# The last join of a triangular inverse: four quadrant products per head rewritten as products over all 128 rows and columns, with one kept tile

## The chip, the core and the metric

The kernel runs on one core of one Trainium2 chip, in one launch. The metric is the time of that launch in device microseconds, the lower the better. Before the change three runs gave 2576.31, 2579.31 and 2580.29 us; the median is 2579.31 us.

Five engines take part, each with its own instruction queue worked off in order: TensorE (PE in the profile; its weight loads are listed apart as PEld), VectorE (DVE), ScalarE (ACT), GpSimd (POOL), and SyncE (SP), which issues the DMA transfers. They meet through semaphores: an instruction that needs another engine's result waits in its queue until the semaphore has the value.

## What is computed

One layer of a hybrid network over 128 context tokens and 2048 latent tokens (17 tiles of 128), width 1024: a normalised and modulated input goes through one projection into a gated DeltaNet in two directions (4 heads of 128) and a gated MLP over groups, then through an output projection, and after that through a squared-ReLU MLP of width 4096. The change touches the DeltaNet alone. The reference solves a unit lower triangular system for each chunk and head:

```python
k_beta = k * beta
a_mat = jnp.where(strict, jnp.einsum('bnhcd,bnhsd->bnhcs', k_beta, k) * decay, 0.0)
rhs = jnp.concatenate([v * beta, k_beta * jnp.exp(g)[..., None]], axis=-1)
sol = lax.linalg.triangular_solve(a_mat + jnp.eye(DN_CHUNK, dtype=f32), rhs,
                                  left_side=True, lower=True, unit_diagonal=True)
```

The kernel works on chunks of 128 tokens and forms the inverse of this matrix itself, with matrix products.

## The kernel before

The work falls into three stretches. Up to about 430 us the kernel projects the tokens, convolves and normalises queries and keys, and writes them and their products to DRAM. From there to about 1230 us it runs the DeltaNet scan with the remaining projections between its steps. The rest is the MLP, almost all of it 128x512 products on PE (helper `mm3`, L220 to L222: each product of two float32 matrices is done as three products of high and low parts).

**The scan.** There are 34 units (one tile of 128 tokens in one direction: context forward and backward, 16 latent tiles forward, 16 backward), each with four heads. `unit` has the steps that follow the state from unit to unit ("chain"). Two successive units form a `pair`, and `pair` holds the steps that need no state ("prep"): the inverse for the eight heads of the pair at once. So there are 17 pairs; only the first mixes directions, and in the other 16 all eight heads have the same one.

**The inverse.** `AH` is minus the system matrix in half precision, and `AL` what half precision left out. `X` and `Y` are the approximate inverse and its transpose, built up from diagonal blocks: `firsts` starts with blocks of 2, and `level(w)` for w = 2, 4, 8, 16, 32 joins neighbouring blocks of w to blocks of 2w. A level is two steps. The first multiplies `AH` with half of the columns of `Y` (L1173: eight products, each with a 128x128 stationary operand and 64 moving columns) and DVE puts the result under a mask into the tile `P` of that level (L1176). The second multiplies `X` with `P` (L1187) and `P` with `X` (L1193), eight products each, again 128x128 with 64 moving columns, and ACT copies both results back into `Y` and `X` (L1196).

The last join, from blocks of 64 to the whole 128, is written apart, and on quadrants. `rows[d]` names for direction d the half `ra` and the half `rb` of the rows. Step one (L1212) multiplies the 64x64 quadrant `AH[rb, ra]` with the 64x64 quadrant `Y[rb, rb]`, and ACT copies the result into the first 64 columns of a fresh tile `Pm` (L1215). Step two multiplies the quadrant `X[ra, ra]` with `Pm` (L1224) and `Pm` with `X[ra, ra]` (L1228); ACT copies the first into `Y` (L1231) and DVE the second into `X` (L1232). Two more steps follow: the residual `R` of the inverse in full precision (L1240 to L1242), and one correction with it into `T` (L1249 to L1251), which the chain uses. `Pm` and `R` are two tiles in turn in the same buffer, which has one slot (tag "R").

**The order.** Every step has a due time in units; `emit` writes them down sorted by it, and projection work ("fill") is placed between chain and prep steps. PE executes that list in order: in most places six 128x512 products stand between one step of the chain or the inverse and the next, long enough for the copy that the next step needs.

Of the kernel before, what the change touches and what calls it, by code (L numbers as in the profile page):

```python
# [62 lines left out]
def hybrid_step(  # L63
# [7 lines left out]
    V, A, G, T = nc.vector, nc.scalar, nc.gpsimd, nc.tensor  # L71
# [73 lines left out]
    def bc4(ap):  # L145
        return ap.unsqueeze(1).to_broadcast([P, 4, P])
# [780 lines left out]
    with ExitStack() as ph:  # L927
# [8 lines left out]
        def pd():  # L936
            return psd.tile([P, 4, P], F32, tag="d", name="pd", bufs=4)
# [7 lines left out]
        def pd8():  # L945
            return psd.tile([P, 8, 64], F32, tag="d", name="pd", bufs=4)

        def f16(tag):
            return pp.tile([P, 8, P], F16, tag=tag, name=tag, bufs=1)
# [12 lines left out]
        def clear(lo, hi):  # L962
            for pm in pms.values():
                V.tensor_copy(pm[:, lo:hi], ident16.unsqueeze(1).to_broadcast([P, hi - lo, P]))

        clear(0, 8)

        def behind(fn, name):

            start = len(tc.nc.cur_bb.bb.instructions)  # L970
            fn()
            for x in tc.nc.cur_bb.bb.instructions[start:]:
                tc.add_manual_dep(x, name, mybir.DependencyInfo(
                    mybir.DependencyClass.NoSync, mybir.DependencyReason.DATA), reason="order")
# [144 lines left out]
        def pair(us):  # L1119

            g = {}
            ds = [u["d"] for u in us]
            spans = [(0, 8, ds[0])] if ds[0] == ds[1] else [(0, 4, ds[0]), (4, 8, ds[1])]
# [4 lines left out]
            def mine(name, c):  # L1128
                return g[name][:, 4 * c : 4 * c + 4, :]
# [73 lines left out]
            rows = {d: (slice(64 * d, 64 * d + 64), slice(64 - 64 * d, P - 64 * d)) for d in (0, 1)}  # L1203

            @steps.append
            def _():
                p = pd8()
                g["Pm"] = f16("R")
                for lo, hi, d in spans:
                    ra, rb = rows[d]  # L1210
                    for h in range(lo, hi):
                        T.matmul(p[ra, h, :], g["AH"][rb, h, ra], g["Y"][rb, h, rb], start=True, stop=True)  # L1212
                for lo, hi, d in spans:
                    ra, rb = rows[d]
                    A.copy(g["Pm"][ra, lo:hi, 0:64], p[ra, lo:hi, :])  # L1215

            @steps.append
            def _():
                py, px = pd8(), pd8()
                pm = g["Pm"]  # L1220
                for lo, hi, d in spans:
                    ra, rb = rows[d]
                    for h in range(lo, hi):
                        T.matmul(py[ra, h, :], g["X"][ra, h, ra], pm[ra, h, 0:64], start=True, stop=True)  # L1224
                for lo, hi, d in spans:
                    ra, rb = rows[d]
                    for h in range(lo, hi):
                        T.matmul(px[rb, h, :], pm[ra, h, 0:64], g["X"][ra, h, ra], start=True, stop=True)  # L1228
                for lo, hi, d in spans:
                    ra, rb = rows[d]  # L1230
                    A.copy(g["Y"][ra, lo:hi, rb], py[ra, lo:hi, :])  # L1231
                    V.tensor_copy(g["X"][rb, lo:hi, ra], px[rb, lo:hi, :])  # L1232

            @steps.append
            def _():
                g["R"] = f16("R")
                for c in range(2):
                    p = pd()
                    for h in range(H):
                        T.matmul(p[:, h, :], mine("AH", c)[:, h, :], mine("Y", c)[:, h, :], start=True, stop=False)  # L1240
                        T.matmul(p[:, h, :], mine("AL", c)[:, h, :], mine("Y", c)[:, h, :], start=False, stop=True)
                    V.tensor_tensor(out=mine("R", c), in0=p, in1=bc4(ident16), op=ALU.add)  # L1242
# [619 lines left out]
    rows = {}  # L1862
# [7 lines left out]
    def final(t, y):  # L1870

        ga = gate_rows(0) if t == 0 else rows["ga"]
        x = [fetch(x2_d[t * P : (t + 1) * P, n * 512 : n * 512 + 512], "x") for n in range(2)]
        ss = smp.tile([P, 2], F32, tag="ss2", name="ss2")
        half_out(y, 1, x, ga, ss)

        def rest():
            half_out(y, 0, x, ga, ss)
            r = smp.tile([P, 1], F32, tag="r", name="r")
            add(ss[:, 0:1], ss[:, 0:1], ss[:, 1:2])  # L1880
            rsqrt_cols(r, ss[:, 0:1], 1, 1.0 / D, EPS)
            for n in range(2):
                V.scalar_tensor_tensor(out=y[n], in0=y[n], scalar=r, in1=rows["nf"][n], op0=ALU.mult, op1=ALU.mult)
                store(out=yrow(t)[:, n * 512 : n * 512 + 512], in_=y[n])

        return rest
# [88 lines left out]
    for j, t in enumerate(range(8, -1, -1)):  # L1975
        st = h2_steps(t, bank, lambda: junk16, w512, own=own_tile if t == 0 else None)
        p = 16 + 19 * j // 2
# [43 lines left out]
    for m, (n, i, u, q) in enumerate(todo):  # L2021
# [6 lines left out]
        if q == 0:  # L2028
            ps = bank()
            if i == 4:  # L2030
                rest = final(pairs[u][1], [acc["v", u], acc["q", u]])
            elif i == 2:
                rest = final(0, [y0[0], y0[1]]) if u == 8 else final(pairs[u][0], [acc["x", u], acc["u", u]])
        h, lo = sops.pop(m)
# [75 lines left out]
```

## Time and profile before

| what | value |
|---|---|
| three runs | 2576.31, 2579.31, 2580.29 us |
| span of the profiled execution, first to last instruction | 2574.7 us |
| PE busy in the span | 2542.1 us, 99%, 15296 products |
| DVE, ACT, POOL busy | 1781.9, 1192.5, 313.9 us |
| mean granted TensorE clock | 0.999 |
| first and last start of L1212, L1224, L1228 | 494.7 and 1182.0 us |

The page lists no time of the profiled execution beside its span. The span is 4.6 us below the median of the runs (0.18%) and 1.6 us below the fastest of them, so it belongs to a run like these, and what an execution holds ahead of its first and behind its last instruction is small. In the timeline each row has the start and the length in us, the engine, the source line, the result and the operands, the rows and columns of the array that the stationary operand takes (64\*64, 128\*128), the shape of the moving operand and its type, and the number of instructions merged into the row; a bracket has the idle time before it and what ended it. A product is pipelined, so its length overlaps the next one: what PE spends on it is the distance from its start to the next start.

### The profile page before, as it was taken

To read this page: it belongs to the slowest core of one execution; us is meant where nothing else is said; L and a number is where in the kernel's file an instruction comes from. 1 tells how busy PE (TensorE), PEld (TensorE's weight loads), DVE (VectorE), ACT (ScalarE), POOL (GpSimd) and SP (SyncE) were. 2 spreads that over 40 slices of the span, in tenths; PEclk is the share of its full clock that TensorE was granted. 3 is DMA by queue.
4 is the path that set the end of the run, shared out by engine and by line. 5 is a ranking of instruction groups with operands and counts; after the bars stand their busy time and mean duration, and the time that the engine had idled before them with its cause. 6 is when DMAs were issued, how large, how long until landed. Compare 5 with 4: busy or idle time off the path is not lost.

```text
span 2574.7 us, 43713 instructions
## 1 busy us (share of the span) xinstructions
PE 2542.1 (99%) x15296; PEld 2134.4 (83%) x15296; DVE 1781.9 (69%) x3524; ACT 1192.5 (46%) x2758; POOL 313.9 (12%) x512
## 2 busy tenths in 40 slices
PE   8999999999999999999999999999999999999998
PEld 4999999788888778888888888888888888888887
DVE  5777746666667788885587887677674445675874
ACT  4755555554545556763355553333243333243441
POOL 3112112222222233331000000000000000000000
PEclk9999999999999999999999999999999999999999
DMA  8966637755555758896778798445599878786773
GB/s 293 297 221 208 197 118 231 235 165 168 165 168 177 229 185 261 280 311 209 268 219 252 214 292 284 140 144 155 177 298 310 279 261 301 238 258 212 232 251 107
DMA packets 533859, 579.77 MB, mean 225 GB/s; under 512 B 35500, under 2 KB 366684, under 8 KB 530054
## 3 DMA queue, kind: packets, MB, share of 16 engines
q1 hardware_dynamic: 533638, 576.98, 70.5%
q8 instruction: 120, 1.97, 0.3%
q14 instruction: 101, 0.83, 0.1%
HBM read 397.62 MB, written 179.22 MB: 224 GB/s over the span
## 4 chain that ended last, share of the span: by engine, by line
PE 55%; DVE 1%; issue 1%; DMA 0%; ACT 0%; POOL 0%; SPq 0%; DVEq 0%; POOLq 0%; ACTq 0%
PE f L220 17%; PE f L221 17%; PE f L222 17%; PE pj L220 1%; PE pj L222 1%; PE pj L221 1%; PE f L856 0%; PE pd L992 0%; PE pd L1096 0%; PE pd L1097 0%; DMA gr<-g_d 0%; PE pm L1418 0%; DMA x<-in_x_sample_dram 0%; PE pd L1060 0%; PE f L270 0%
## 5 line engine op out<-in xcount | busy, mean ns | idle before, releaser
L220 PE MATMUL f<-hop,zH 128*128 128x512 f32 x960 | 373.2, 389 | 0.0
L222 PE MATMUL f<-hop,zL 128*128 128x512 f32 x960 | 373.1, 389 | 0.0
L221 PE MATMUL f<-hop,zH 128*128 128x512 f32 x960 | 373.1, 389 | 0.0
L220 PE MATMUL f<-hop,wH 128*128 128x512 f32 x896 | 351.5, 393 | 0.0
L221 PE MATMUL f<-hop,wH 128*128 128x512 f32 x896 | 348.9, 390 | 0.0
L222 PE MATMUL f<-hop,wL 128*128 128x512 f32 x896 | 344.3, 390 | 0.0
L1604 ACT CAST zH<-zraw 128x512 fp32r<-128x512 f32 x240 | 146.5, 620 | 296.0 <-DMA zraw<-s_d 92.7
L1598 DVE TENSOR_TENSOR zL<-zraw,zH 128x512 fp32r<-128x512 f32 x240 | 162.1, 687 | 72.7 <-ACT zH L1604 61.6
L220 PEld LDWEIGHTS f<-hop,zH 128*128 128x128 f32 x960 | 180.3, 188 | 37.3
L222 PEld LDWEIGHTS f<-hop,zL 128*128 128x128 f32 x960 | 180.2, 188 | 37.3
L221 PEld LDWEIGHTS f<-hop,zH 128*128 128x128 f32 x960 | 180.2, 188 | 37.3
L222 PEld LDWEIGHTS f<-hop,wL 128*128 128x128 f32 x896 | 168.2, 188 | 35.6
L220 PEld LDWEIGHTS f<-hop,wH 128*128 128x128 f32 x896 | 168.5, 188 | 34.1 <-issue 0.9
L221 PEld LDWEIGHTS f<-hop,wH 128*128 128x128 f32 x896 | 168.6, 188 | 32.2
L222 PE MATMUL pj<-kH,wL 128*128 128x386 f32 (+2 forms) x568 | 190.6, 335 | 0.0
L220 PE MATMUL pj<-kH,wH 128*128 128x386 f32 (+2 forms) x568 | 189.1, 336 | 0.3 <-DVE kH L487 0.3
L221 PE MATMUL pj<-kL,wH 128*128 128x386 f32 (+2 forms) x568 | 189.3, 333 | 0.0
L178 POOL TENSOR_TENSOR r<-rsq,nhalf 128x1 f32<-128x1 f32 (+1 forms) x38 | 22.3, 587 | 1352.4 <-DVE rsq L177 1352.4
L1751 ACT CAST wH<-s 128x512 fp32r<-128x512 f32 x96 | 58.9, 620 | 172.8 <-DVE s L1598 157.3
L537 DVE SCALAR_TENSOR_TENSOR cv<-pj,vec,cv 128x384 f32<-128x384 f32 (+2 forms) x164 | 87.1, 538 | 58.4 <-ACT cv L534 57.0
L220 PEld LDWEIGHTS pj<-kH,wH 128*128 128x128 f32 x568 | 107.1, 189 | 4.9 <-issue 4.4
L221 PEld LDWEIGHTS pj<-kL,wH 128*128 128x128 f32 x568 | 107.4, 189 | 0.6
(408 smaller groups left out, 5729.3 us busy)
## 6 DMA issues: line engine op xcount, KB each, us to landing
zraw<-z_d SPq DMA_DIRECT2D x212, 256.0 KB
raw<-in_w_ff_dram SPq DMA_DIRECT2D x128, 256.0 KB
hop<-hop_d SPq DMA_DIRECT2D x28, 1024.0 KB
z_d<-c SPq DMA_DIRECT2D x96, 256.0 KB
zraw<-s_d SPq DMA_DIRECT2D x96, 256.0 KB
raw<-in_w_mod_dram SPq DMA_DIRECT2D x80, 256.0 KB
r<-in_w_ff_dram SPq DMA_DIRECT2D x80, 256.0 KB
s_d<-s SPq DMA_DIRECT2D x64, 256.0 KB
```

The source lines that it names most:

```text
L178: G.tensor_tensor(out=out, in0=t[:np_, :n], in1=nhalf[:np_, :n], op=ALU.pow)
L220: T.matmul(ps, lh, rh, start=first and i == 0, stop=False, skip_group_check=more)
L221: T.matmul(ps, lh, rl, start=False, stop=False, skip_group_check=more)
L222: T.matmul(ps, ll, rh, start=False, stop=last and i == n - 1, skip_group_check=more)
L537: V.scalar_tensor_tensor(out=cv[:, o : o + m], in0=ps[:, s + sh : s + sh + m], scalar=convw[:, w, j : j + 1], in1=cv[:, o : o + m], op0=AL ...
L1598: V.tensor_tensor(out=out, in0=a, in1=b, op=op)
L1604: A.copy(h, src)
L1751: A.copy(h, s2)
```

## The change

The three groups of products in the last join go over all 128 rows. Step one has the whole of `AH` as stationary operand and the 64 columns `rb` of `Y` in all 128 rows; of the result only the rows `ra` are copied out, as before. They go into the columns `rb` of one tile `rest`, which is allocated once for all pairs and cleared once with a memset on DVE. Step two has the whole of `X` as stationary operand and the 64 columns `rb` of `rest`, and then the whole of `rest` as stationary operand and the 64 columns `ra` of `X`. The rows and columns that come in beside the old quadrants meet blocks of `X` and `Y` that are still zero at that point, so the parts that are copied out are the same. The residual `R` is written into `rest` too, over the intermediate.

```diff
@@ -964,6 +964,8 @@
         clear(0, 8)
+        rest = f16("R")
+        V.memset(rest, 0.0)
@@ -1205,27 +1207,22 @@
                 p = pd8()
-                g["Pm"] = f16("R")
+                for lo, hi, d in spans:
+                    for h in range(lo, hi):
+                        T.matmul(p[:, h, :], g["AH"][:, h, :], g["Y"][:, h, rows[d][1]], start=True, stop=True)
                 for lo, hi, d in spans:
                     ra, rb = rows[d]
-                    for h in range(lo, hi):
-                        T.matmul(p[ra, h, :], g["AH"][rb, h, ra], g["Y"][rb, h, rb], start=True, stop=True)
-                for lo, hi, d in spans:
-                    ra, rb = rows[d]
-                    A.copy(g["Pm"][ra, lo:hi, 0:64], p[ra, lo:hi, :])
+                    A.copy(rest[ra, lo:hi, rb], p[ra, lo:hi, :])
 
             @steps.append
             def _():
                 py, px = pd8(), pd8()
-                pm = g["Pm"]
                 for lo, hi, d in spans:
-                    ra, rb = rows[d]
                     for h in range(lo, hi):
-                        T.matmul(py[ra, h, :], g["X"][ra, h, ra], pm[ra, h, 0:64], start=True, stop=True)
+                        T.matmul(py[:, h, :], g["X"][:, h, :], rest[:, h, rows[d][1]], start=True, stop=True)
                 for lo, hi, d in spans:
-                    ra, rb = rows[d]
                     for h in range(lo, hi):
-                        T.matmul(px[rb, h, :], pm[ra, h, 0:64], g["X"][ra, h, ra], start=True, stop=True)
+                        T.matmul(px[:, h, :], rest[:, h, :], g["X"][:, h, rows[d][0]], start=True, stop=True)
@@ -1233,7 +1230,7 @@
-                g["R"] = f16("R")
+                g["R"] = rest
```

The lines behind the memset shift by two, those behind the last join go back by three; L1212, L1224 and L1228 of before are L1212, L1222 and L1225 of the change. But for these numbers, the order of the instructions on every engine is what it was, with the memset as the one new row, and each PE instruction waits for the same instruction as before. On PE, at the first group of the second pair, before (the pattern repeats for eight heads):

```order
L222 MATMUL pm<-wH,hL 128x512
L992 MATMUL pd<-vn,kt 128x128 x4
L1212 LDWEIGHTS AH
L1212 MATMUL pd<-Y,AH 64x64
```

and in the change:

```order
L222 MATMUL pm<-wH,hL 128x512
L994 MATMUL pd<-vn,kt 128x128 x4
L1212 LDWEIGHTS AH
L1212 MATMUL pd<-Y,AH 128x64
```

Only the shape moved: the moving operand has 128 rows in place of 64, for the same 64 columns. On DVE, ahead of the first pair, in the change, with the semaphores (of DMA queues, PE and ACT) that each instruction waits for:

```order
L964 COPY P_5735<-ident_179 128x1024 [waits PE_49]
L964 COPY P_5736<-ident_179 128x1024
L968 MEMSET R 128x512 [waits DMAHW4_49,DMAHW7_49,DMAHW1_49,DMAHW0_49]
L1298 SCALAR_TENSOR_TENSOR th<-th,pj 128x512 [waits Activation_49]
```

The memset stands between the five copies that fill the tiles `P` and a gate product (L1301 of before, L1298 of the change). It waits for DMA transfers that still read the memory which the tile takes over from the first stretch.

## Prediction

> **What bounds the kernel now.** First the page's line of busy times; then the busy times by stretch (PEclk is the granted clock).
>
> ```profile
> PE 2542.1 (99%) x15296; PEld 2134.4 (83%) x15296; DVE 1781.9 (69%) x3524; ACT 1192.5 (46%) x2758; POOL 313.9 (12%) x512
> ```
>
> ```profile
> core 0: us, PE busy (x) PEld busy (x) DVE busy (x) ACT busy (x) POOL busy (x), PEclk, DMA share, GB/s
> ...
> 494.00:700.00 206.00, 203.43 (x1799) 167.06 (x1798) 137.38 (x355) 104.41 (x232) 46.14 (x55) 1.00 0.54 160
> 700.00:950.00 250.00, 244.28 (x2144) 201.85 (x2143) 189.29 (x474) 130.72 (x298) 61.80 (x69) 1.00 0.64 194
> 950.00:1190.00 240.00, 234.76 (x2119) 194.00 (x2115) 198.25 (x433) 161.07 (x427) 83.56 (x73) 1.00 0.83 259
> 1190.00:1900.00 710.00, 710.00 (x3383) 592.12 (x3382) 520.08 (x862) 293.61 (x587) 7.23 (x11) 1.00 0.69 220
> ```
>
> PE works without a break at full clock. In the stretch where the changed groups run (about 494 to 1190 us) it is idle for 2.6, 5.7 and 5.2 us; behind it not at all up to 1900 us. So what PE gains there moves everything behind it forward, save where PE then waits for DVE or ACT. Being busy says nothing of how well: the question is what PE spends on the changed products, from one start to the next.
>
> **The products, small and whole.** The kernel holds its own comparison. The levels L1173, L1187 and L1193 already have the form that the change gives to L1212, L1224 and L1228. From the groups by form (the last two lines of the join have the same count as the first, 136):
>
> ```profile
> L1173 PE MATMUL pd<-Y,AH 128*128 128x64 f16 x640 | 32.4, 193 | 0.0
> ...
> L1212 PE MATMUL pd<-Y,AH 64*64 64x64 f16 x136 | 7.6, 195 | 0.4 <-ACT Y L1196 0.4
> ```
>
> By the length of one product, 193 against 195 ns, nothing would change. But these lengths overlap, and the distances between starts tell another thing. One pair in PE's timeline, first a level's group of eight, then the group of eight of the last join:
>
> ```profile
> 781.31 0.40 PE L222 MATMUL pj<-wH,hL 128*128 128x512 f32 x1
> 781.55 0.41 PE L1173 MATMUL pd<-Y,AH 128*128 128x64 f16 x8
> 781.79 0.47 PE L220 MATMUL pj<-wH,hH 128*128 128x512 f32 x1
> 782.11 0.39 PE L221 MATMUL pj<-wL,hH 128*128 128x512 f32 x1
> ...
> 786.76 0.40 PE L222 MATMUL pj<-wH,hL 128*128 128x512 f32 x1
> 787.09 0.43 PE L1212 MATMUL pd<-Y,AH 64*64 64x64 f16 x8
> 787.45 0.50 PE L220 MATMUL pj<-wH,hH 128*128 128x512 f32 x1
> 787.79 0.40 PE L221 MATMUL pj<-wL,hH 128*128 128x512 f32 x1
> ```
>
> From the product ahead of the group to the second one behind it, the whole array takes 782.11 - 781.31 = 0.80 us, the quadrants 787.79 - 786.76 = 1.03 us. Of the 0.23 us, 0.09 lie ahead of the group (0.33 against 0.24), 0.12 between its start and the next (0.36 against 0.24), and 0.02 in the step behind that (0.34 against 0.32). Now the group of sixteen, L1187 with L1193 against L1224 with L1228:
>
> ```profile
> 573.91 0.40 PE L222 MATMUL pj<-wH,hL 128*128 128x512 f32 x1
> 574.15 0.41 PE L1187 MATMUL pd<-P,X 128*128 128x64 f16 x8
> 574.39 0.40 PE L1193 MATMUL pd<-X,P 128*128 128x64 f16 x8
> 574.63 0.47 PE L220 MATMUL pj<-wH,hH 128*128 128x512 f32 x1
> 574.94 0.40 PE L221 MATMUL pj<-wL,hH 128*128 128x512 f32 x1
> ...
> 788.72 0.39 PE L222 MATMUL pj<-wH,hL 128*128 128x512 f32 x1
> 789.04 0.34 PE L1224 MATMUL pd<-R,X 64*64 64x64 f16 x5
> 789.19 0.21 PE L1228 MATMUL pd<-X,R 64*64 64x64 f16 x1
> ...
> 789.30 0.32 PE L1228 MATMUL pd<-X,R 64*64 64x64 f16 x5
> 789.55 0.50 PE L220 MATMUL pm<-wH,hH 128*128 128x512 f32 x1
> 789.89 0.39 PE L221 MATMUL pm<-wL,hH 128*128 128x512 f32 x1
> ```
>
> Whole array: 574.94 - 573.91 = 1.03 us. Quadrants: 789.89 - 788.72 = 1.17 us. Here the small form wins something back: a product with `R` as weights starts 0.15 us after the first with `X` while those still run, since they take different quadrants, and all sixteen fit into 0.51 us in spite of what is lost on leaving them. Still it is 0.14 us longer in sum.
>
> So the loss sits at the borders: PE pauses for some 0.09 us when it goes from 128x128 to a smaller piece, and again on the way back. The first stretch of the kernel shows the way back for another small form, a transpose that takes 32 rows:
>
> ```profile
> 66.11 0.37 PE L617 MATMUL pt<-ident,absb 32*128 32x32 f32 x3
> 66.41 0.44 PE L221 MATMUL pj<-kL,wH 128*128 128x388 f32 x1
> ```
>
> ```profile
> L617 PE MATMUL pt<-ident,absb x17: 220/222/249, 66.1 to 396.1; 32*128 32x32 f32 x17
> ```
>
> The row of three lasts 0.37 us and one of them 0.22 (the middle one of shortest, median and longest in ns), so the third starts near 66.26, 0.15 us ahead of the next product, while the three stand 0.075 us apart. The Trainium skill, "TensorEngine Tiling (Array Packing)", section "Key Properties", says that a change of tiling mode, not only of tile, drains TensorE; the rows above agree, with 0.09 us each way.
>
> **The change part by part.** *The products.* Sixteen pairs of one direction: 0.23 us in the group of eight and 0.14 in that of sixteen, 0.37 x 16 = 5.9 us. The first pair mixes directions and has its products in three groups; I put it at a pair's 0.37. Sum 6.3 us. The bounds: with the borders alone, 4 x 0.09 x 17 = 6.1 us; without them (the pause belongs to the place, not to the form) only the inner difference is left, below.
>
> *The copies* L1215, L1231 and L1232 read and write as many elements as before, L1215 into another half of the columns: nothing either way; the six 128x512 products ahead of L1224 (787.45 to 788.72 and its successor) cover L1215 as they did.
>
> *The kept tile.* The buffer had one slot before, so the copy into it had to wait for the same readers; each PE instruction waits for the same one as before. Nothing.
>
> *The memset.* It stands on DVE between these rows:
>
> ```profile
> 445.04 1.76 DVE L964 COPY P<-ident 128x1024 f16<-128x1024 f16 x5
> 449.81 0.69 DVE L1301 SCALAR_TENSOR_TENSOR th<-th,pj 128x512 f32<-128x512 f32 x1 [3.02 <-ACT th L1300]
> ```
>
> It writes as much as one of the five copies, 1.76/5 = 0.35 us, and at most the 0.69 us of a 128x512 float operation. DVE stands idle for 3.02 us there, waiting for ACT, and that covers it. Without the cover it would cost its 0.35 to 0.69 us once. Queued behind it are L1301 and, through the PSUM bank that this frees, PE's fill.
>
> *What is not passed on.* In three places another engine holds PE behind a changed group. From PE's timeline:
>
> ```profile
> 870.73 0.41 PE L1212 MATMUL pd<-Y,AH 64*64 64x64 f16 x8 [0.38 <-ACT Y L1196]
> ...
> 920.80 0.43 PE L1212 MATMUL pd<-Y,AH 64*64 64x64 f16 x8
> ...
> 923.02 0.50 PE L221 MATMUL pj<-wL,oH 128*128 128x512 f32 x1 [0.65 <-DVE wL L192]
> ...
> 1138.74 0.43 PE L1212 MATMUL pd<-Y,AH 64*64 64x64 f16 x8
> ```
>
> and in the chain that ended last:
>
> ```profile
> 1130.34 0.30 DVE o L1403
> ...
> 1160.60 0.67 DVE P L1176
> ...
> 1161.31 0.41 PE pd L1187 x8
> ```
>
> After 870.73 PE waits again for ACT's copy, which stands in a busy ACT queue, so the gain of that group of eight (0.23) goes; the wait at 923.02, for a weight split on DVE, follows the group of eight at 920.80 and eats another 0.23. The chain that ended last runs over DVE, with a few pieces of ACT, from 1130.34 to 1161.31, past the pair at 1138.74, and eats its 0.37 whole. Elsewhere DVE itself waits for PE between the group and the next place where PE waits for it, and moves with it. Lost: 0.23 + 0.23 + 0.37 = 0.8 us, and I take 0.9 for smaller cases.
>
> The sum: 6.3 - 0.9 = 5.4 us. The span goes from 2574.7 to 2569.3 us. The median of the runs stands 4.6 us above that span, so by it 2579.3 - 5.4 = 2573.9 us.
>
> **The rivals.** *The gain is eaten by the scan's other engines.* For it: DVE is busy for 198.25 of the 240 us from 950 on, and the only chain shown there is DVE's. Against it: the same stretch shows DVE waiting for PE in most pairs. If all six pairs behind 950 us gave nothing and half of the six between 700 and 950, what is left is 6.3 - 9 x 0.37 = 3.0 us: 2576.3 us.
>
> *The pause belongs to the place* (a wait for ACT ahead of each group), and the full form only loses the overlap of quadrants. Then a pair saves about 0.03 in the group of eight (its starts span 0.24 us now with eight whole products, and 0.36 - 0.09 = 0.27 with quadrants) and loses some 0.06 in the sixteen (0.48 against 0.51 - 0.09 = 0.42): 0.03 x 17 = 0.5 us slower, 2579.8 us. Against it: the levels wait for ACT as well (L1173 reads the `Y` that L1196 copies) and show no pause. The Trainium skill, same page, section "Theoretical Speedup", promises up to 2x for each dimension of 64 or less, which speaks against leaving the quadrants; the trace gives 0.42 against 0.48 us, as just worked out, and more than that back at the borders.
>
> *Slower: the memset holds DVE.* It waits for transfers of the first stretch. ACT's timeline a little later:
>
> ```profile
> 454.22 1.28 ACT L1019 ACTIVATE gr<-gr,gcol 128x128 f32<-128x128 f32 x4 [4.44 <-DMA gr<-g_d]
> ```
>
> ACT stood idle there for 4.4 us for a load, so landings are late in this stretch. If they come after 449.2 us or so, the gate product behind it comes late, its PSUM bank stays taken, and PE's fill stops once its other banks are full. Each further microsecond then costs up to one; beyond 5.4 us, that is with a landing after about 455 us, the change loses. With 3 us more it is 2582 us. Against it: the transfers concerned were issued before the five copies ran.
>
> **How the numbers follow.** The forecast has 0.57, the eaten gain 0.31, the pause of the place 0.07, the memset 0.05. 0.2% is 5.2 us, about what a measurement of this kernel can tell from no change; the forecast of 5.4 lies almost on that bound. Within it the sum is uncertain by some 1 us and the median by about as much (the three runs spread over 4.0 us), so I give it 0.5 of its 0.57 for faster and the rest for the same; a little of the eaten gain comes out faster by chance. Faster 0.52, same 0.43, slower 0.05. The range: from 2579.3 - 6.3 - 2.0 = 2571 us (all passed on, in a low median) to 2577.5 us, which holds most of the eaten gain; the pause and the memset are left out.
>
> **What would show it.** In the changed profile L1212, L1222 and L1225 stand as 128\*128; the step from L222 to the first of a group is 0.24 us, not 0.33, the group of eight ends after 0.24 us, that of sixteen after 0.48. PE's idle time in the three stretches grows by 0.9 us in sum if the losses are as said, by 3.3 if that rival holds. The memset shows as one row near 446.8 us. Wrong it would be if the steps at the borders stayed at 0.33 and 0.36, or if they shrank and the span did not.

## The result, and the profile after

The changed kernel takes 2573.71 us (median of 21 runs, 2569.93 to 2576.11), the kernel before, run beside it, 2577.61 us (21 runs, 2574.75 to 2582.12). The ratio is 0.9981, with a 95% interval of 0.9975 to 0.9987: 4.9 us faster (3.4 to 6.4). The two medians lie 3.9 us apart, within that interval. Two later comparisons of the same kernels, told below, gave 0.9984 and 0.9987.

The profiled execution has a span of 2572.3 us and took 2574.06. From its page, busy times as before:

```profile
PE 2536.5 (99%) x15296; PEld 2132.5 (83%) x15296; DVE 1782.1 (69%) x3525; ACT 1192.8 (46%) x2758; POOL 315.1 (12%) x512
```

The busy times of the scan by stretch (us, then PE, PEld, DVE, ACT, POOL, each with its count):

```profile
494.00:700.00 206.00, 202.85 (x1803) 167.46 (x1803) 139.05 (x361) 104.05 (x230) 45.98 (x56) 1.00 0.52 161
700.00:950.00 250.00, 244.79 (x2177) 203.59 (x2174) 189.88 (x479) 133.52 (x306) 64.13 (x70) 1.00 0.62 195
950.00:1190.00 240.00, 233.41 (x2109) 193.66 (x2108) 199.15 (x438) 158.99 (x423) 82.36 (x71) 1.00 0.82 259
```

PE is idle there for 3.15, 5.21 and 6.59 us, 14.95 in sum, against 13.53 before. So PE spends less on its products, and some of that comes back as waiting; the last stretch alone has 1.35 us more. The two groups in PE's timeline, at the same pair as in the prediction:

```profile
786.56 0.40 PE L222 MATMUL pj<-wH,hL 128*128 128x512 f32 x1
786.80 0.41 PE L1212 MATMUL pd<-Y,AH 128*128 128x64 f16 x8
787.04 0.47 PE L220 MATMUL pj<-wH,hH 128*128 128x512 f32 x1
787.35 0.39 PE L221 MATMUL pj<-wL,hH 128*128 128x512 f32 x1
...
788.27 0.40 PE L222 MATMUL pj<-wH,hL 128*128 128x512 f32 x1
788.51 0.41 PE L1222 MATMUL pd<-R,X 128*128 128x64 f16 x8
788.75 0.40 PE L1225 MATMUL pd<-X,R 128*128 128x64 f16 x8
788.99 0.47 PE L220 MATMUL pm<-wH,hH 128*128 128x512 f32 x1
789.30 0.39 PE L221 MATMUL pm<-wL,hH 128*128 128x512 f32 x1
```

From the product ahead to the second one behind, the eight take 787.35 - 786.56 = 0.79 us (1.03 before) and the sixteen 789.30 - 788.27 = 1.03 us (1.17 before): the levels' distances, as forecast. The first product starts 0.24 us behind L222, not 0.33.

**Where the gain goes.** The PE instructions of the two executions match one to one, so the distance of each can be compared. From the first group of a level at 485 us on, the groups of eight save 4.1 us in sum and those of sixteen 1.9. PE's lead, the time by which it needs less from that group to the same instruction behind the scan (at 1460 us in the kernel before), is 4.3 us. Ahead of 485 us this execution lost 2.0 us against the other one, 1.75 of it ahead of the memset, where nothing was changed; that is why the spans differ by 2.4 us and not by 4.3. Over all the profiled executions of this document PE comes to that group between 482.2 and 487.0 us, so the start alone spreads by as much as the change is worth.

Two places take most of it back in this execution; smaller losses elsewhere (0.49 us at 526.8, 0.35 at 586.6) and gains (0.2 to 0.3 each at 915, 921 and 942 us) nearly cancel. The first place is the copy L1215 of the intermediate. ACT's timeline, and below it PE's, at a late pair:

```profile
1002.81 0.64 ACT L1022 ACTIVATE gr<-gr 128x512 f32<-128x512 f32 x1
1003.34 0.61 ACT L874 CAST opH<-d 128x512 fp32r<-128x512 f32 x1
1003.98 0.58 ACT L1215 CAST R<-pd 64x512 f16<-64x512 f32 x1
```

```profile
1002.71 0.41 PE L1212 MATMUL pd<-Y,AH 128*128 128x64 f16 x8
...
1004.19 0.40 PE L222 MATMUL pj<-wH,oL 128*128 128x512 f32 x1
1004.61 0.39 PE L1222 MATMUL pd<-R,X 128*128 128x64 f16 x8
```

ACT works without a gap and ends the copy at 1003.98 + 0.58 = 1004.56 us; PE starts L1222 at 1004.61, 0.42 us behind the product ahead and not 0.24. The same pair before:

```profile
1006.40 0.58 ACT L1215 CAST R<-pd 64x512 f16<-64x512 f32 x1
```

```profile
1005.20 0.43 PE L1212 MATMUL pd<-Y,AH 64*64 64x64 f16 x8
...
1007.15 0.34 PE L1224 MATMUL pd<-R,X 64*64 64x64 f16 x5
```

There the copy ended at 1006.98, 0.17 us ahead of its reader. Before, L1224 came 1.95 us after L1212; with the group of eight shortened it could come after 1.71, and the copy, held in ACT's queue, ends 1.85 us after L1212. Four pairs show this (871.94, 1004.61, 1049.08, 1093.54 us): they change by +0.10, +0.01, +0.04 and +0.04 us in the group of sixteen where the others gain 0.15, in sum 0.8 us. In the first of them the copy had no cover left even before: from L1212 to the first of the sixteen it is 2.13 us in both kernels.

The second place is at 1144 us. The rows of ACT, DVE and PE in the changed kernel's timeline there:

```profile
1142.50 0.62 ACT L874 CAST opH<-y 128x512 fp32r<-128x512 f32 x1 [4.09 <-DMA hop_d<-opH]
...
1143.28 0.69 DVE L875 TENSOR_TENSOR opL<-y,opH 128x512 fp32r<-128x512 f32 x1 [1.40 <-DMA hop_d<-opL]
...
1143.89 1.28 DVE L1239 TENSOR_TENSOR R<-pd,ident 128x512 f16<-128x512 f32 x2
...
1144.63 0.38 PE L1246 MATMUL pd<-R,X 128*128 128x128 f16 x4 [1.06 <-DVE R L1239]
```

ACT and DVE split the scan's output into halves (`opH` L874, `opL` L875) that a store then carries away; these tiles come from a ring of four, and a new one has to wait until the store of an older one has landed. The wait stands in both queues, and DVE's residual L1239, which PE waits for, stands behind it. It costs PE 1.6 us. The first of the two DVE rows before:

```profile
1145.07 0.69 DVE L875 TENSOR_TENSOR opL<-y,opH 128x512 fp32r<-128x512 f32 x1 [0.15 <-DMA hop_d<-opL]
```

The store cost DVE 0.15 us there, and PE, which came to it later, nothing.

That the shorter groups bring this wait about is not shown. A kernel of the experiments that is as slow as the one before (64 rows of the array) has it too, and PE loses 1.2 us to it. In its timeline, where L1255 is the L1246 of above and L1248 the L1239:

```profile
1145.49 0.69 DVE L875 TENSOR_TENSOR opL<-y,opH 128x512 fp32r<-128x512 f32 x1 [1.44 <-DMA hop_d<-opL]
...
1146.84 0.38 PE L1255 MATMUL pd<-R,X 128*128 128x128 f16 x4 [0.64 <-DVE R L1248]
```

### The profile page after: what moved, and what is told of

Read it like the earlier page. It is cut to its first block, busy times and chain, and to the rows that moved or that the text cites. A ratio compares the mean times of both kernels' runs of the same rounds, so it can differ in the third digit from the quotient of the medians.

```text
span 2572.3 us, 43717 instructions
## 1 busy us (share of the span) xinstructions
PE 2536.5 (99%) x15296; PEld 2132.5 (83%) x15296; DVE 1782.1 (69%) x3525; ACT 1192.8 (46%) x2758; POOL 315.1 (12%) x512
## 4 chain that ended last, share of the span: by engine, by line
PE 55%; DVE 1%; issue 1%; DMA 0%; ACT 0%; POOL 0%; DVEq 0%; POOLq 0%; ACTq 0%
PE f L220 17%; PE f L221 17%; PE f L222 17%; PE pj L220 1%; PE pj L222 1%; PE pj L221 1%; PE f L856 0%; PE pd L994 0%; PE pd L1098 0%; PE pd L1099 0%; DMA hop_d<-opL 0%; PE pm L1415 0%; PE pd L1062 0%; PE f L270 0%; PE f L1738 0%
## 5 line engine op out<-in xcount | busy, mean ns | idle before, releaser
L220 PE MATMUL f<-hop,zH 128*128 128x512 f32 x960 | 373.2, 389 | 0.0
L222 PE MATMUL f<-hop,zL 128*128 128x512 f32 x960 | 373.1, 389 | 0.0
L220 PE MATMUL f<-hop,wH 128*128 128x512 f32 x896 | 351.4, 393 | 0.0
L222 PE MATMUL f<-hop,wL 128*128 128x512 f32 x896 | 344.3, 390 | 0.0
L222 PEld LDWEIGHTS f<-hop,zL 128*128 128x128 f32 x960 | 180.2, 188 | 37.4
L220 PEld LDWEIGHTS f<-hop,zH 128*128 128x128 f32 x960 | 180.2, 188 | 37.3
L222 PEld LDWEIGHTS f<-hop,wL 128*128 128x128 f32 x896 | 168.2, 188 | 35.7
L220 PEld LDWEIGHTS f<-hop,wH 128*128 128x128 f32 x896 | 168.5, 188 | 33.9 <-issue 0.9
L222 PE MATMUL pj<-kH,wL 128*128 128x386 f32 (+2 forms) x568 | 190.5, 335 | 0.0
L220 PE MATMUL pj<-kH,wH 128*128 128x386 f32 (+2 forms) x568 | 189.2, 336 | 0.5 <-DVE kH L487 0.3
L220 PEld LDWEIGHTS pj<-kH,wH 128*128 128x128 f32 x568 | 107.1, 189 | 5.1 <-issue 4.7
```

What stands on the lines that cost most here:

```text
L220: T.matmul(ps, lh, rh, start=first and i == 0, stop=False, skip_group_check=more)
L222: T.matmul(ps, ll, rh, start=False, stop=last and i == n - 1, skip_group_check=more)
```

## The experiments

None of them leaves out or changes part of what is computed. "Steps" are medians of PE's distances between starts, in ns, worked out from the traces; those of the eight are over the six pairs where a group of eight stands between a product of the chain and L220, those of the sixteen over the six pairs where it stands between L222 and L220.

| kernel | eight: entry, within, exit, next | sum | sixteen: entry, within, exit, next | sum |
|---|---|---|---|---|
| before (quadrants 64x64) | 205, 242, 123, 337 | 907 | 318, 396, 122, 338 | 1175 |
| changed (128x128) | 112, 203, 29, 314 | 659 | 230, 448, 29, 313 | 1020 |
| only the eight whole | 111, 204, 29, 315 | 659 | 319, 396, 123, 338 | 1175 |
| only the sixteen whole | 205, 243, 123, 337 | 907 | 230, 448, 29, 313 | 1020 |
| 128 rows, 64 columns | 205, 243, 126, 335 | 909 | 327, 396, 126, 338 | 1187 |
| 64 rows, 128 columns | 208, 213, 120, 340 | 881 | 320, 447, 120, 335 | 1222 |
| 128 rows, 96 columns | 112, 298, 45, 315 | 770 | (half of the products) | |

### The two halves of the change

```diff
-T.matmul(py[:, h, :], g["X"][:, h, :], rest[:, h, rows[d][1]], start=True, stop=True)
+T.matmul(py[rows[d][0], h, :], g["X"][rows[d][0], h, rows[d][0]], rest[rows[d][0], h, rows[d][1]], start=True, stop=True)
-T.matmul(px[:, h, :], rest[:, h, :], g["X"][:, h, rows[d][0]], start=True, stop=True)
+T.matmul(px[rows[d][1], h, :], rest[rows[d][0], h, rows[d][1]], g["X"][rows[d][0], h, rows[d][0]], start=True, stop=True)
```

> Only the group of eight (L1212) takes the whole array; the sixteen products of L1222 and L1225 are 64x64 quadrants again; memset, kept tile and copies as in the changed kernel. Border theory (PE pauses some 0.09 us each time it goes from 128x128 to a smaller form and back): L222 to the second product behind the group of eight takes 0.80 us in sum, that behind the group of sixteen 1.17 us as before the change; PE gains 0.23 x 17 = 3.9 us, of which the same places as in the changed kernel eat 1 to 2 us, so 2 to 3 us faster than before (ratio 0.9988 to 0.9992). Rival, that the pause belongs to the place: the group of eight stays near 1.03 us and the time is that of before within 0.5 us. Rival, that the gain comes from the kept tile and not from the products: 4 to 5 us faster, as the changed kernel.

```diff
-T.matmul(p[:, h, :], g["AH"][:, h, :], g["Y"][:, h, rows[d][1]], start=True, stop=True)
+T.matmul(p[rows[d][0], h, :], g["AH"][rows[d][1], h, rows[d][0]], g["Y"][rows[d][1], h, rows[d][1]], start=True, stop=True)
```

> The other half: the sixteen products (L1222, L1225) take the whole array, the group of eight (L1212) is of quadrants again. Border theory: 1.02 us for the sixteen instead of 1.17, and 1.03 for the eight as before: PE gains 0.14 x 17 = 2.4 us, of which 1 us or less is eaten: 1.4 to 2.4 us faster than before (ratio 0.9991 to 0.9995). If the two halves add up, the two gains over before sum to the 4.9 us of the changed kernel. Rival, pause of the place with only the overlap lost: 0.06 x 17 = 1.0 us slower than before.

Measured: with the eight alone 2575.35 us, ratio 0.9989 (0.9980 to 0.9998), 2.8 us faster; with the sixteen alone 2574.76 us, 0.9991 (0.9982 to 1.0000), 2.3 us faster. The intervals are wide, but the steps are exact: in the table's pairs each half moves its own group and leaves the other's within 1 ns. In PE's lead between 485 and 1460 us the halves have 2.6 and 1.8 us, the whole 4.3. The pause follows the products and not the place: the rival that puts it down to a wait at that place falls.

The two halves also settle where the loss at the copy L1215 comes from. In PE's timeline of the kernel with the eight alone, at the late pair shown above:

```profile
1005.10 0.40 PE L222 MATMUL pj<-wH,oL 128*128 128x512 f32 x1
1005.54 0.31 PE L1222 MATMUL pd<-R,X 64*64 64x64 f16 x5
```

The sixteen are quadrants as before, but they start 0.44 us behind L222 and not 0.33; in all four pairs named above this group takes 0.07 to 0.14 us longer than before. With the sixteen alone, where the group of eight is as long as before, they start after 0.23 us there, and the last three of those pairs gain their whole 0.15 us. So it is the shorter group of eight that uncovers the copy.

### Which side of the array makes the pause

```diff
-T.matmul(p[:, h, :], g["AH"][:, h, :], g["Y"][:, h, rows[d][1]], start=True, stop=True)
+T.matmul(p[rows[d][0], h, :], g["AH"][:, h, rows[d][0]], g["Y"][:, h, rows[d][1]], start=True, stop=True)
```

(and the same in the other two groups)

> All three groups use all 128 rows of the array but only 64 of its columns (weights 128x64); the same values come out, since the rows added are zeros of the block-triangular operands. It asks which dimension of the form makes PE pause at the border. If any smaller form pauses: L222 to the group 0.33 us, group to the next product 0.12 us behind the last, so 1.03 us for the eight and 1.20 for the sixteen: 6.2 us of PE lost against the changed kernel, 0 to 1 us slower than before. If only the rows count (the transposes of 128 rows by 8 columns at L687 enter after 0.11 us as wholes do): 0.80 and 1.02 us, the time of the changed kernel within 1 us. I hold the second for the likelier, 0.6 to 0.4.

```diff
-T.matmul(p[:, h, :], g["AH"][:, h, :], g["Y"][:, h, rows[d][1]], start=True, stop=True)
+if ds[0] == ds[1]:
+    T.matmul(p[:, h, :], g["AH"][rows[d][1], h, :], g["Y"][rows[d][1], h, rows[d][1]], start=True, stop=True)
+else:
+    T.matmul(p[:, h, :], g["AH"][:, h, :], g["Y"][:, h, rows[d][1]], start=True, stop=True)
```

(and the same in the other two groups)

> All three groups of the sixteen pairs of one direction use 64 rows of the array and all 128 columns (weights 64x128); the one pair of mixed directions stays whole. If the rows make the pause: L222 to the group 0.33 us, 0.09 us lost again behind it, 1.03 us for the eight and 1.20 for the sixteen: (0.23 + 0.18) x 16 = 6.6 us of PE lost against the changed kernel, the time of before or up to 1 us slower. If only the columns make it: 0.80 and 1.02 us and the time of the changed kernel within 1 us. If any smaller form pauses, this kernel and the one of 64 columns are both as slow as before.

Measured: 64 columns 2577.02 us, ratio 1.0000 (0.9991 to 1.0009); 64 rows 2578.01 us, ratio 1.0000 (0.9991 to 1.0009). Both are as slow as before; the guess that only the rows count was wrong. One pair with 64 columns in PE's timeline:

```profile
788.60 0.40 PE L222 MATMUL pj<-wH,hL 128*128 128x512 f32 x1
788.93 0.44 PE L1212 MATMUL pd<-Y,AH 128*64 128x64 f16 x8
789.30 0.50 PE L220 MATMUL pj<-wH,hH 128*128 128x512 f32 x1
```

The pause is 0.09 us ahead and 0.09 us behind whichever side is halved: here the entry is 788.93 - 788.60 = 0.33 us, and the table has 208 and 205 ns against 112, and 120 and 126 against 29. The overlap comes from the columns: with 64 columns sixteen products fit into 396 ns as with quadrants, with 64 rows they need 447 as with the whole array. That says nothing against rows: with 64 columns the second eight lie in the other half of the columns, but no form here puts them in another half of the rows than the first eight. Summed over both groups 64 rows take the longest of the four forms (2.10 us; quadrants 2.08), but the times don't part them.

```diff
-T.matmul(p[:, h, :], g["AH"][:, h, :], g["Y"][:, h, rows[d][1]], start=True, stop=True)
+n = 96 if ds == [0, 0] else P
+T.matmul(p[0:n, h, :], g["AH"][:, h, 0:n], g["Y"][:, h, rows[d][1]], start=True, stop=True)
```

(and the same with `X` in the first eight of the sixteen)

> In the pairs where both blocks run in the first direction, the group of eight and the first eight of the sixteen use 96 columns of the array, with all 128 rows; the rest is as in the changed kernel. With 64 columns the border cost 0.09 us each way; with 8 columns (L687, one instruction) it did not show. If any number of columns below 128 costs the pause: L222 to the group 0.33 us, 0.12 us behind it. If it belongs to a tile of 64 or less and not to the number itself: 0.24 and 0.03 us, as with 128. I hold the second for likelier, 0.7 to 0.3. The time of one look can't tell the two apart; the steps can.

Measured: one time, 2572.20 us. PE's timeline of this kernel:

```profile
784.04 0.39 PE L222 MATMUL pj<-wH,hL 128*128 128x512 f32 x1
784.26 0.51 PE L1213 MATMUL pd<-Y,AH 128*96 128x64 f16 x8
784.61 0.47 PE L220 MATMUL pj<-wH,hH 128*128 128x512 f32 x1
```

With 96 columns there is no pause: PE enters after 0.22 us and leaves after 45 ns, about one step of the group. The pause belongs to a form of 64 (or, at L617, of 32 rows), not to any number below 128. The one product of 8 columns (L687, at 437.21 us before) has none either, with 109 ns in and 29 out; which other widths pause was not measured. But the eight products themselves stand 298/7 = 43 ns apart, not 29. The weight loads of the group of eight, by form, in the 96-column kernel:

```profile
L1213 PEld LDWEIGHTS <-AH 128*96 128x96 f16 x64 | 4.1, 125 | 0.3
...
L1213 PEld LDWEIGHTS <-AH 128*128 128x128 f16 x72 | 2.8, 98 | 2.9 <-issue 2.9
```

and with 64 rows:

```profile
L1213 PEld LDWEIGHTS <-AH 64*128 64x128 f16 x128 | 4.6, 95 | 4.5 <-issue 3.8
```

A load of 128 columns takes 95 to 98 ns, with 64 rows or 128; one of 96 columns takes 125 (one of 64 columns 112, a quadrant's 108). The Trainium skill, "TensorE: Matmul & The Clock Gate", section "Weight-path perf modes", says that the fast weight load is on when there are 128 weights and the type is not FP32; these rows agree in the order. The load is not what makes the pause: with 64 rows it takes 95 ns and PE pauses, with 96 columns it takes 125 and PE doesn't.

### The kept tile alone

```diff
 (all three groups as quadrants, on the kept tile)
+T.matmul(p[rows[d][0], h, :], g["AH"][rows[d][1], h, rows[d][0]], g["Y"][rows[d][1], h, rows[d][1]], start=True, stop=True)
```

> All three groups are 64x64 quadrants as before; only the kept tile, its memset and the copy into the other half of the columns stay. Theory (kept tile and memset cost nothing and bring nothing): the time of before within 0.5 us. If the two halves of the change each already contained a gain of the kept tile (their gains of 2.8 and 2.4 us sum to a little more than the 4.1 to 4.9 us of the whole), it is up to 1 us faster; if the memset holds DVE, slower.

Measured: 2577.36 us, ratio 1.0001 (0.9992 to 1.0010). The steps are those of before, and the time is the same within 2.3 us either way; no gain of the kept tile shows, and the two halves account for the whole. In its profile PE is 0.8 us behind the kernel before at 1460 us, nearly all of it lost at 937 and 944 us.

### The changed kernel again

> The changed kernel unaltered, once more, beside the next two on the same chip. Asked: are the places where its gain goes those of the first profile? If they are: PE waits for the residual (L1246 <- DVE R L1239) for 1 to 2 us near 1145 us, with ACT standing over 3 us ahead of it for the store hop_d<-opH, and PE is later than in the kernel before by no more at 1140 us than 4 to 6 us of lead say, whatever the start-up gives. If the stall was a chance of one execution, it is below 0.3 us here, and the span is 1 to 1.5 us shorter against PE's place at 485 us than in the first profile. Time: 4 to 6 us faster than before.

> The changed kernel unaltered, a third time, as the neighbour of the other three on this chip: 4 to 5 us faster than before. In its profile PE's waits between 900 and 1150 us, summed, again leave about 4.3 us of the 6.7 that the groups save, if what eats the gain is not one place but the other engines' and the transfers' schedule there.

Measured: 2573.43 us, ratio 0.9984 (0.9975 to 0.9992), and 2574.03 us, 0.9987 (0.9978 to 0.9996): 4.1 and 3.4 us. PE's lead from 485 to 1460 us is 4.3 and 4.6 us, as in the first profile (4.3). But the losses lie elsewhere in each. In the second execution PE loses only 0.4 us at 1145 us, and about 1.0 us here (its PE timeline):

```profile
937.55 0.66 PE L1415 MATMUL pm<-ident,o 128*128 128x128 f32 x4 [0.61 <-DVE o L1400]
...
944.55 0.40 PE L1189 MATMUL pd<-P,X 128*128 128x64 f16 x8 [0.29 <-DVE P L1178]
```

where the first had no wait. In the third it is 1.0 us at 1143 us. So the stall for the store is neither a chance of one execution nor a constant: it takes 0.4 to 1.6 us. The three lists of losses (0.8 us for the copy L1215 in each, and 1.7, 1.6 and 1.4 us for all the rest) are much the same in sum. The third kernel's expectation for the lead, about 4.3 of 6.7 us, held; its time, 3.4 us faster, was to be 4 to 5.

The rest can't all be charged to the change. Kernels that gain nothing lose at the same places against the one profile of before: 0.7 us each at 937 and 944 us with 64 columns and with the kept tile alone, 1.2 us at the store with 64 rows. From 485 to 1460 us PE is 0.4, 0.8 and 0.4 us behind in these three. So the 0.8 us of the copy is the change's, and how much of the other 1.4 to 1.7 is, stays open.

### More room for the half tiles

```diff
 def fhalf(name, dt):
-    return sp.tile([P, 512], dt, tag="raw", name=name)
+    return w512(name, dt)
```

> The changed kernel with one more edit: the tiles of an earlier block's halves (fhalf, which ACT and DVE fill at L874 and L875 and a store empties) come from the larger pool of weights and not from the ring of four raw slots, so that ACT need not wait for the store of the half four tiles back. All computation is the same. Theory (the gain is lost at 1145 us to that store: ACT's L874 waits 4.09 us, DVE's L875 and L1239 behind it, and PE 1.23 + 0.38 us): PE's wait for R near 1145 us falls below 0.3 us, and the time is 1.0 to 1.6 us below that of the changed kernel, so 5.5 to 6.5 us below before (ratio 0.9975 to 0.9979). Rival (behind the store the chain of DVE takes over at once, or the weight pool's own loads come later and PE waits for them): the time is that of the changed kernel within 0.5 us, or above it.

> The same edit of the half tiles on the kernel before, with quadrants. Theory: there the store's wait (2.47 us of ACT, 0.15 us of DVE) was covered by PE's later arrival, and PE waited for R no longer than 0.4 us, so the edit alone is worth 0 to 0.4 us (ratio 0.9998 to 1.0000). Rival, that the edit helps for reasons of its own (transfers, other slots): it is worth 1 us or more here too, and then says nothing of the join.

> The changed kernel with the half tiles from the weight pool, a second time, since its first interval (0.9968 to 0.9986) does not part it from the changed kernel's. If the edit is worth what the medians of the first time said (2 us): again 1 us or more below the changed kernel beside it. If only run-to-run spread: within 1 us of it, on either side.

Measured: on the changed kernel 2571.37 us, ratio 0.9977 (0.9968 to 0.9986), and the second time 2572.59 us, 0.9980 (0.9971 to 0.9989); on the kernel before 2577.84 us, 1.0004 (0.9995 to 1.0013), where no gain shows. On the changed kernel the medians lie 2.1 and 1.4 us below its unedited neighbour, and the intervals overlap with that one's: the sign came out alike twice, but the size, and a gain at all, are not settled. What happened to the wait is plain. PE's start of L1246 at 1145 us now follows without a wait, but in the list of PE's waits (us in total, times, longest)

```profile
PE pj L1415 <- DVE o L1400: 3.8, 3, 1.3
```

of the changed kernel turned, with the edit, into

```profile
PE pj L1415 <- DMA ob<-ob_d: 4.9, 3, 1.9
```

The half tiles now sit in the pool that the load of `ob` needs a slot of, and the load comes late. PE's lead at 1460 us in the two profiles is 4.0 and 3.7 us, no more than without the edit. The theory's first half holds, the 1.0 to 1.6 us that were to come from it don't show in the profiles.

```diff
 def fhalf(name, dt):
-    return sp.tile([P, 512], dt, tag="raw", name=name)
+    return hp.tile([P, 512], dt, tag="h", name=name)
```

> The changed kernel with the half tiles in another ring, the eight tiles of the last stage's halves, where no weight waits for a slot; three groups of six products change places with products of the last join's residual, nothing else of PE's order. If the slots of the raw ring are what holds ACT at 1142 us: PE's wait for R there is below 0.3 us, and the time 1 to 1.5 us below the changed kernel beside it. If the waits move elsewhere, as the waits for the load of ob did in the weight pool's version (3 of 1.5 to 2.1 us), the time is the changed kernel's within 0.7 us.

Measured: 2569.11 us (six runs, 2567.73 to 2573.08), ratio 0.9970 (0.9959 to 0.9982): 7.7 us faster than before, and by the medians 4.9 us faster than the changed kernel beside it (2574.03); the two intervals against before just overlap (0.9982 and 0.9978). By the medians it is the fastest version here. PE's wait for R is 0.16 us, as the theory had it, but most of the gain comes from a place that it had not named. In the changed kernel, at 1022 us (and again at 1067 and 1111 us), PE's timeline and DVE's:

```profile
1022.12 0.66 PE L1415 MATMUL pj<-ident,o 128*128 128x128 f32 x4 [1.24 <-DVE o L1400]
```

```profile
1018.40 2.02 DVE L849 TENSOR_SCALAR x<-x,r 128x512 f32<-128x512 f32 x2 [0.36 <-POOL r L178]
1020.34 0.68 DVE L1438 TENSOR_TENSOR x<-x,tmp 128x512 f32<-128x512 f32 x1
1020.94 1.13 DVE L1400 SCALAR_TENSOR_TENSOR o<-o,rr,ga 128x128 f32<-128x128 f32 x4
```

and PE's and DVE's with the half tiles in this other ring:

```profile
1018.34 0.60 PE L1415 MATMUL pj<-ident,o 128*128 128x128 f32 x4
```

```profile
1015.42 0.35 DVE L1400 SCALAR_TENSOR_TENSOR o<-o,rr,ga 128x128 f32<-128x128 f32 x1
1015.68 0.68 DVE L1437 TENSOR_TENSOR tmp<-pj,row 128x512 f32<-128x512 f32 x1
1016.28 1.67 DVE L1400 SCALAR_TENSOR_TENSOR o<-o,rr,ga 128x128 f32<-128x128 f32 x3
```

DVE has `o` done ahead of L1438 and no longer waits for POOL in front of it, and PE gains about 2.6 us between 1005 and 1137 us. The edit changes the slots, with them the order that comes out for DVE, and PE's order at three places (1008, 1052 and 1097 us of the changed kernel), in the same stretch. Which of these brings it was not parted. It has nothing to do with the join: the kernel before has the same three waits, the first of them here, 3.8 us in sum as in the changed one.

```profile
1024.74 0.66 PE L1418 MATMUL pj<-ident,o 128*128 128x128 f32 x4 [1.24 <-DVE o L1403]
```

The edit was not tried on the kernel before, so what it is worth there is open.

## Why the prediction was right, and where its steps were not

The time was forecast at 2573.9 us and came out at 2573.7. That is closer than the steps deserve: the base of 2579.3 us was the median of three runs, and 21 runs put it at 2577.6, 1.7 us lower; the gain of 5.4 us was too large by 0.5 to 2.0 us (3.4 to 4.9 measured). By the medians it is 3.9 us, 1.5 less than forecast, and the two errors nearly cancel. That is luck. The prediction took 0.2%, 5.2 us, for what can be told from no change and gave 0.52 to a gain beyond it; the gain is smaller than that, yet 21 runs of each do tell it from none.

*The products.* Right: 0.80 and 1.03 us were read from the levels, 0.79 and 1.03 came; the pauses of 0.09 us are gone at both ends. The groups save 4.1 and 1.9 us, and with the 0.8 lost at the copies it is some 6.7 us in 17 pairs (6.3 forecast). Too wide was only that PE pauses for any "smaller piece": 96 columns don't pause.

*The copies.* This step failed. It put L1215 at nothing since "the six 128x512 products ahead of L1224 cover L1215 as they did". They are the same six, but the cover is measured from L1212, and the change shortens L1212's own group by 0.24 us. In most pairs the copy starts when PE is done, and the cover holds. In three pairs where ACT's queue is full the copy ended 0.17 us ahead of its reader, and now PE waits about as long for it: 0.5 us that the sum had at nothing. The fourth, at 870.73 us, it had in the next term.

*What is not passed on.* The term was mis-sized, and of its three places one is as forecast. Behind 870.73 us PE waits for ACT's copy as said, and the group's 0.23 us goes there (0.25 with the sixteen's part). At 923.02 us nothing was lost: the wait became shorter (0.65 to 0.35 us). The pair at 1138.74 us was to lose its 0.37; 0.4, 1.0 and 1.6 us went right behind it in the three executions, at the store of a half tile, which that view of the chain had not shown as a limit and which stalls a kernel without the gain too. All in all 2.1 to 2.4 us of the 6.7 did not arrive, not 0.9; 0.8 of them are the copies'.

*The kept tile and the memset.* Right. The memset stands at 448.14 us, right behind the copies (446.33 + 1.76 = 448.09), with 0.48 us (0.35 to 0.69 forecast), and DVE still waits 2.48 us behind it:

```profile
448.14 0.48 DVE L968 MEMSET R<- 128x512 uint32 x1
451.11 0.69 DVE L1298 SCALAR_TENSOR_TENSOR th<-th,pj 128x512 f32<-128x512 f32 x1 [2.48 <-ACT th L1297]
```

*The rivals.* That the scan's other engines eat the gain is half true: PE does wait more for them, in the stretch it named, but 2.1 to 2.4 us are gone and not 3.3, and not all of that is shown to come from the change. PE's idle time grew by 1.4 us, between the 0.9 of the forecast and the 3.3 of the rival, and the gain of 3.4 to 4.9 us lies between the rival's 3.0 and the forecast's 5.4. A chance of 0.31 was not too much for it. That the pause belongs to the place is refuted by the two halves and by the forms of 64, and that the memset holds DVE by the rows above and the kept tile alone.

## What to carry to other kernels

Price small products by the distances between starts, with the step into the group and the step out of it, never by their own length: here eight and sixteen quadrant products between full-array products lost 0.2 us a group at the borders, more than their overlap won. When a group on the bounding engine gets shorter, whatever it covered on another queue loses that much cover; go through each copy that starts behind the group and see whether its engine is free at that moment. Before a loss is put down to the change, look whether a kernel that gains nothing loses it too. And take the base from many runs where the change is as small as their spread.

## What the runs showed of the hardware that was not expected

Halving the rows or the columns of the array gives the same pause of 0.09 us each way, and 96 columns give none. That agrees with the Trainium skill, "TensorEngine Tiling (Array Packing)", section "Key Properties", where it is the change of tiling mode that drains TensorE: 96 columns are in none of the modes that the same page lists under "Available Configurations". Overlap came only where the two eights lay in different halves of the columns (396 against 447 ns for sixteen); different halves of the rows were not tried. And a stationary operand of 64 or 96 columns loads more slowly, 108 to 125 ns against 95 to 98; the group of eight with 96 columns takes 0.11 us more than with 128 (770 against 659 ns), which goes with the slower load, though no run parts the two.
